# Batched x·yᵀ over 96 heads: all loads first, then 24 stores of four heads, and matmuls of 64 columns

## The chip, the cores and the metric

The kernel runs on one core of one Trainium2 chip. The time is the device time of one execution in microseconds. Before the change it is 300.93 us, the median of 3 runs (300.91 to 301.05).

The core has a matrix engine (PE, its weight loads are shown as PEld), a vector engine (DVE), a scalar engine (ACT), a general engine (POOL), an engine that here only issues transfers (SP), and 16 DMA engines that move data between DRAM and the on-chip memory. Matmul results arrive in PSUM, and DVE or ACT copies them from there.

## The reference

```
x, y: [batch 8, heads 12, 512, channels 64], float32
out = einsum('bhtc,bhsc->bhts', x, y)          # [8, 12, 512, 512], float32
```

For each of the 96 heads a 512x64 matrix is multiplied by the transpose of another. The inputs are 12.6 MB each and the output is 100.7 MB.

## The kernel before

**Tiling.** The 96 heads are taken in NG = 6 groups of G = 16 heads. A group of x (or y) is one load of 2 MB into a slot of 128 partitions x 4096 float32; there are five such slots (SLOTS), which hold the loads first and the results later. Load number n is x of group n/2 for even n, and y for odd n: 12 loads in all. Each group is worked on in two halves of eight heads (NH = 12 halves, numbered i = 2g + half), and each half gives four results of two heads (result, o = 4i + h): 128 partitions x 8 rows x 512 columns, 2 MB, written by one store in rows of 16 KB. There are 48 stores.

**From a load to the matmul's operands.** Everything that follows is counted in bfloat16.
- compress(n) for x: ACT casts the whole slot into a buffer xk (line 113 of the helper copy).
- compress(n) for y: four casts of 64 partitions x 2048 elements into the buffers yb, two for each half. The list in_front gives their engines: DVE and POOL for the first half, DVE and ACT for the second (line 150).
- mix(i, name, part): four copies of 32 partitions x 2048 from xk into xb. In xb two neighbouring 16-bit columns belong to different heads, and each partition fills only one of the two; the other keeps the zero of a memset made once. So one contraction over all 128 partitions yields rows of two heads, each with its own channels. There is one xb for each half (xbs, line 64).
- transposes(i): DVE transposes xb to xT and yb to yT in blocks of 32x32 (lines 178 and 188). There are two buffers of each, one for each half.
- result(o): for each of two groups of four rows (k = 0 and 4) four matmuls of 128 columns by 512 into a PSUM tile pm of four banks (line 202), and one copy of 128x2048 from pm to the slot (line 113), on ACT except in the two results named in late, where DVE makes it.
- store(o): issued by SP, or by ACT for every third result and for the last four (by_act).

**Order and waits.** The program is written out by hand. emit notes for each buffer who wrote and who read it last and adds the semaphore waits that follow; each engine and each DMA queue works strictly in its own order, so that what stands behind a waiting instruction waits too. The front (lines 246 to 271) issues five loads, then goes through the 12 loads and compresses each; POOL makes one mix copy after each of them (12 in all, for i = 0, 1, 2). Later loads follow when a slot is free, the first four results are put between the last loads, and afterwards prepare makes the transposes of half i and the mix of half i + 1 on DVE while the results of earlier halves are stored.

Of the kernel before, what the change touches and what calls it, by code (L numbers as in the profile page):

```python
# [9 lines left out]
def kernel(  # L10
# [22 lines left out]
    nc = tc.nc  # L33
    B, H, T, C = x.shape
    _, _, S, _ = y.shape
    P = 128
    G = 16
    Q = P // G
    R = T // Q
    NG = B * H // G  # L40
    NH = 2 * NG
    V = G // 4
    K = 8
    E = R // K
    D = 32
    SLOTS = 5
    fp32 = mybir.dt.float32
    bf16 = mybir.dt.bfloat16
    u32 = mybir.dt.uint32
    COPY = mybir.ActivationFunctionType.Copy  # L50
    assert C == 2 * D and S == T and R == 2 * D and Q * V == D

    xv = x.rearrange("b h t c -> (b h t c)").rearrange("(g p n) -> g p n", p=P, n=R * C)
    yv = y.rearrange("b h t c -> (b h t c)").rearrange("(g p n) -> g p n", p=P, n=R * C)
    ov = out.rearrange("b h t s -> (b h t s)").rearrange(
        "(o u h q n) -> o h q u n", u=2, h=V, q=Q * E, n=K * S
    )

    sb = ctx.enter_context(tc.tile_pool(name="sb", bufs=1))
    ps = ctx.enter_context(tc.tile_pool(name="ps", bufs=1, space=bass.MemoryType.PSUM))  # L60
    slots = [sb.tile([P, K * S], fp32, name=f"slot{i}") for i in range(SLOTS)]
    xks = [sb.tile([P, R, C], bf16, name=f"xk{i}") for i in range(NG - 1)]
    ybs = [[sb.tile([P, R // 2 * D], u32, name=f"yb{h}{i}") for i in range(NG - 1 + h)] for h in range(2)]
    xbs = [sb.tile([P, K * E * D], u32, name=f"xb{half}") for half in range(2)]
    xTs = [sb.tile([P, K * D * E], u32, name=f"xT{i}") for i in range(2)]
    yTs = [sb.tile([P, D * R // 2], u32, name=f"yT{i}") for i in range(2)]
    pms = [ps.tile([P, 4, S], fp32, name=f"pm{i}") for i in range(2)]
# [3 lines left out]
    def need(name, points):  # L71

        best = {}
        for p, v in points:
            if known[name].get(p, 0) < v:
                best[p] = max(best.get(p, 0), v)
        for p, v in list(best.items()):
            if any(snaps[q, w].get(p, 0) >= v for q, w in best.items() if q != p):
                del best[p]
        for p, v in best.items():  # L80
            engines[name].wait_ge(sems[p], v)  # L81
            known[name][p] = v
            for q, w in snaps[p, v].items():
                known[name][q] = max(known[name].get(q, 0), w)
# [19 lines left out]
        for w in writes:  # L104
            writer[w], readers[w] = at, []

    made_slots, loaded, later, late = [], {}, [], (V * NH - V - 1, V * NH - 1)
    in_front = ["dve", "pool", "dve", "act"]

    def copy(name, dst, src, reads, writes):  # L110
        emit(
            name,
            lambda: nc.scalar.activation(dst, src, COPY)  # L113
            if name == "act"
            else engines[name].tensor_copy(dst, src),  # L115
            reads,
            writes,
        )

    def both(i):  # L120
        return [("slot", i, 0), ("slot", i, 1)]

    def slot():
        made_slots.append(len(made_slots) % SLOTS)
        return made_slots[-1]

    def load(n):
        i = loaded[n] = slot()
        emit(
            "sp",  # L130
            lambda: nc.sync.dma_start(slots[i], (yv if n % 2 else xv)[n // 2]),  # L131
            writes=both(i),
            dma=i,
        )

    def compress(n):

        i = loaded.pop(n)
        g = n // 2
        if n % 2 == 0:  # L140
            xk = g % (NG - 1)
            dst = xks[xk].rearrange("p r c -> p (r c)")
            copy("act", dst, slots[i], both(i), [("xk", xk)])
            return
        ys = slots[i].rearrange("p (r c) -> p r c", c=C)
        for half in range(2):
            b = g % (NG - 1 + half)
            yv2 = ybs[half][b].bitcast(bf16).rearrange("p (j c w) -> p j w c", j=R // 2, w=2)
            for ch in range(2):
                copy(  # L150
                    in_front[2 * half + ch],
                    yv2[ch * 64:(ch + 1) * 64],
                    ys[half * 64:(half + 1) * 64, :, ch * D:(ch + 1) * D].rearrange(
                        "p (j w) c -> p j w c", w=2
                    ),
                    both(i),
                    [("yb", half, b, ch)],
                )

    def mix(i, name, part):  # L160

        g, half = divmod(i, 2)
        ch, u = divmod(part, 2)
        lo = half * 64 + u * D
        xk = g % (NG - 1)
        xv2 = xbs[half].bitcast(bf16).rearrange("p (k e c u) -> p k e c u", k=K, e=E, u=2)
        copy(
            name,
            xv2[part * D:(part + 1) * D, :, :, :, u],
            xks[xk][lo:lo + D, :, ch * D:(ch + 1) * D].rearrange("p (e k) c -> p k e c", k=K),  # L170
            [("xk", xk)],
            [("xb", half, part)],
        )

    def transposes(i):
        g, half = divmod(i, 2)
        b = g % (NG - 1 + half)
        emit(
            "dve",
            lambda: nc.vector.transpose(  # L180
                xTs[half].rearrange("p (k r e) -> p k e r", k=K, e=E),
                xbs[half].rearrange("p (k e c) -> p k e c", k=K, e=E),
            ),
            [("xb", half, part) for part in range(4)],
            [("xT", half)],
        )
        emit(
            "dve",
            lambda: nc.vector.transpose(  # L189
                yTs[half].rearrange("p (r j) -> p j r", r=D),  # L190
                ybs[half][b].rearrange("p (j c) -> p j c", c=D),
            ),
            [("yb", half, b, ch) for ch in range(2)],
            [("yT", half)],
        )

    def products(o, k):
        i, h = divmod(o, V)
        xT = xTs[i % 2].bitcast(bf16).rearrange("p (k h m) -> p k h m", k=K, h=V)
        yT = yTs[i % 2].bitcast(bf16)  # L200
        for j in range(4):
            last = nc.tensor.matmul(  # L202
                pms[k // 4][:, j, :], xT[:, k + j, h, :], yT[:, h * S:(h + 1) * S],
                start=True, stop=True,
            )
        return last

    def by_act(o):
        return o % 3 == 2 or o >= V * NH - V

    def store(o, s):
        i, h = divmod(o, V)
        name = "act" if by_act(o) else "sp"
        emit(
            name,
            lambda: engines[name].dma_start(ov[i, h], slots[s]),
            reads=both(s),
            dma=s,
        )

    def result(o, s):

        ot = slots[s].rearrange("p (r s) -> p r s", s=S)
        for k in range(0, K, 4):
            pm = k // 4
            half = o // V % 2
            emit("pe", lambda: products(o, k), [("xT", half), ("yT", half)], [("pm", pm)])
            copy("dve" if o in late else "act", ot[:, k:k + 4, :], pms[pm], [("pm", pm)], [("slot", s, pm)])
            if k == 0:
                while later:  # L230
                    store(*later.pop())
        if by_act(o):
            later.append((o, s))
        else:
            store(o, s)

    def prepare(i):

        if i < NH:
            transposes(i)  # L240
        if i + 1 < NH:
            for part in range(4):
                mix(i + 1, "dve", part)

    with tc.tile_critical():  # L245
        for g in range(SLOTS):
            load(g)
        for half, name in enumerate(("dve", "pool")):
            emit(
                name,  # L250
                lambda: engines[name].memset(xbs[half], 0.0),  # L251
                writes=[("xb", half, part) for part in range(4)],
            )
        front = []
        for n in range(2 * NG):
            if n == 11:
                result(3, slot())
            compress(n)
            mix(n // 4, "pool", n % 4)
            if n == 4:  # L260
                transposes(0)
            if n < 5:
                load(n + SLOTS)
            elif n in (6, 8):
                load(n // 2 + 7)
            elif n < 10:
                front.append(slot())
            if n > 7 and n < 11:
                result(n - 8, front[n - 8])
            if n == 9:  # L270
                transposes(1)
        prepare(2)
        for o in range(V, V * NH):
            result(o, slot())
            if o % V == V - 1:
                prepare(o // V + 2)
        store(*later.pop())
        for i, name in enumerate(("dve", "pool", "dve", "pe", "act")):
            need(name, [(f"dma{i}", ticks[f"dma{i}"])])


# [28 lines left out]
```

## Time and profile before

| what | value |
|---|---|
| device time, median of 3 runs | 300.93 us |
| span of the profiled execution, first to last instruction | 299.3 us |
| PE busy (384 matmuls) | 131.2 us, 44% |
| DVE busy | 160.8 us, 54% |
| ACT busy | 204.2 us, 68% |
| POOL busy | 56.0 us, 19% |
| DMA | 125.90 MB, 421 GB/s over the span |

The page gives the busy time of each engine as a share of the span; the 40 slices give it in tenths by time, with what the DMA engines moved. The groups give the mean time of one instruction and what ended the idle time before it. Names such as xT<-xb stand for the buffers written and read, without their numbers. The profiled execution is known by its span alone; its device time isn't recorded, and the median of the runs lies 1.6 us above that span.

The bytes are 25.17 MB read and 100.66 MB written. Loads take place from the start to about 63 us, stores from 55 us to the end.

### The profile page before, as it was taken

To read this page: it belongs to the slowest core of one execution; us is meant where nothing else is said; L and a number is where in the kernel's file an instruction comes from. 1 tells how busy PE (TensorE), PEld (TensorE's weight loads), DVE (VectorE), ACT (ScalarE), POOL (GpSimd) and SP (SyncE) were. 2 spreads that over 40 slices of the span, in tenths; PEclk is the share of its full clock that TensorE was granted. 3 is DMA by queue.
4 is the path that set the end of the run, shared out by engine and by line. 5 is a ranking of instruction groups with operands and counts; after the bars stand their busy time and mean duration, and the time that the engine had idled before them with its cause. 6 is when DMAs were issued, how large, how long until landed. Compare 5 with 4: busy or idle time off the path is not lost.

```text
span 299.3 us, 1170 instructions
## 1 busy us (share of the span) xinstructions
PE 131.2 (44%) x384; PEld 35.2 (12%) x384; DVE 160.8 (54%) x77; ACT 204.2 (68%) x105; POOL 56.0 (19%) x23
## 2 busy tenths in 40 slices
PE   0000040557756665454655545464646473755100
PEld 0000010111111111111111111111111111111000
DVE  2167897999839590940946729219276330501400
ACT  1665676999999885677776868595959595459000
POOL 2399999991000000000000000000000000000000
PEclk9999999999599978596859597959597959587755
DMA  7999999999999999999999999999999999999995
GB/s 272 429 427 434 431 425 427 429 431 427 434 434 429 429 431 428 431 434 431 427 434 428 429 434 429 429 427 436 425 425 429 427 434 423 425 423 429 431 431 239
DMA packets 8645, 125.90 MB, mean 421 GB/s; under 512 B 960, under 2 KB 960, under 8 KB 960
## 3 DMA queue, kind: packets, MB, share of 16 engines
q1 hardware_dynamic: 6048, 88.08, 69.3%
q10 hardware_dynamic: 2592, 37.75, 29.6%
q8 instruction: 3, 0.05, 0.1%
q14 instruction: 2, 0.02, 0.0%
HBM read 25.17 MB, written 100.66 MB: 420 GB/s over the span
## 4 chain that ended last, share of the span: by engine, by line
DMA 57%; ACT 22%; PE 7%; issue 4%; DVE 3%; SPq 0%; ACTq 0%
DMA out_dram<-slot 44%; ACT slot L113 19%; DMA slot<-in_y_dram 7%; PE pm L202 7%; DMA slot<-in_x_dram 6%; DVE yb L115 2%; DVE slot L115 1%; ACT xk L113 1%; ACT yb L113 1%; SPq L131 0%; ACTq L81 0%; SPq L305 0%; SPq L245 0%
## 5 line engine op out<-in xcount | busy, mean ns | idle before, releaser
L113 ACT ACTIVATE slot<-pm 128x2048 f32<-128x2048 f32 x92 | 166.6, 1883 | 50.1 <-DMA out_dram<-slot 40.8
L202 PE MATMUL pm<-yT,xT 128*128 128x512 bf16 x384 | 131.2, 485 | 146.6 <-ACT slot L113 108.6
L180 DVE STREAM_TRANSPOSE xT<-xb 128x2048 uint32<-128x2048 uint32 x12 | 46.7, 3890 | 71.0 <-PE pm L202 68.6
L202 PEld LDWEIGHTS pm<-yT,xT 128*128 128x128 bf16 x384 | 35.2, 112 | 242.1 <-ACT slot L113 141.4
L115 DVE COPY xb<-xk 32x2048 bf16<-32x2048 bf16 x36 | 46.9, 1304 | 1.0
L115 DVE CAST yb<-slot 64x2048 bf16<-64x2048 f32 x12 | 36.1, 3012 | 17.0 <-DMA slot<-in_y_dram 16.8
L115 POOL COPY xb<-xk 32x2048 bf16<-32x2048 bf16 x12 | 36.2, 3019 | 10.5 <-ACT xk L113 9.7
L113 ACT ACTIVATE xk<-slot 128x4096 bf16<-128x4096 f32 x6 | 21.7, 3617 | 16.4 <-DMA slot<-in_x_dram 16.4
L115 DVE COPY slot<-pm 128x2048 f32<-128x2048 f32 x4 | 9.0, 2286 | 29.3 <-PE pm L202 29.3
L189 DVE STREAM_TRANSPOSE yT<-yb 128x1024 uint32<-128x1024 uint32 x12 | 23.2, 1932 | 0.0
L113 ACT ACTIVATE yb<-slot 64x2048 bf16<-64x2048 f32 x6 | 14.8, 2461 | 5.1 <-DMA slot<-in_y_dram 5.1
L115 POOL CAST yb<-slot 64x2048 bf16<-64x2048 f32 x6 | 17.8, 2968 | 1.3 <-DMA slot<-in_y_dram 0.8
L251 DVE MEMSET xb<- 128x2048 uint32 x1 | 1.8, 1765 | 1.4 <-SPq L245 1.4
L251 POOL MEMSET xb<- 128x2048 uint32 x1 | 1.8, 1804 | 0.5 <-SPq L245 0.5
L113 ACT ACT_TABLE_LOAD x1 | 1.3, 1283 | 0.9 <-SPq L245 0.9
L294 POOL MEMSET const-float32-0.0<- 128x1 f32 x1 | 0.1, 98 | 0.2 <-issue 0.2
L294 POOL MEMSET const-float32-1.0<- 128x1 f32 x1 | 0.1, 98 | 0.0
L294 POOL MEMSET const-bfloat16-1.0<- 128x1 bf16 x1 | 0.1, 98 | 0.0
L294 POOL MEMSET const-uint8-127<- 128x1 uint8 x1 | 0.1, 97 | 0.0
## 6 DMA issues: line engine op xcount, KB each, us to landing
out_dram<-slot SPq DMA_DIRECT2D x30, 2048.0 KB, 17.0
out_dram<-slot ACTq DMA_DIRECT2D x18, 2048.0 KB, 14.8
slot<-in_x_dram SPq DMA_DIRECT2D x6, 2048.0 KB, 17.6
slot<-in_y_dram SPq DMA_DIRECT2D x6, 2048.0 KB, 20.8
```

Of the source, the lines that this page charges most:

```text
L113: lambda: nc.scalar.activation(dst, src, COPY)
L115: else engines[name].tensor_copy(dst, src),
L180: lambda: nc.vector.transpose(xTs[half].rearrange("p (k r e) -> p k e r", k=K, e=E), xbs[half].rearrange("p (k e c) -> p k e c", k=K, e=E),),
L189: lambda: nc.vector.transpose(yTs[half].rearrange("p (r j) -> p j r", r=D), ybs[half][b].rearrange("p (j c) -> p j c", c=D),),
L202: last = nc.tensor.matmul(pms[k // 4][:, j, :], xT[:, k + j, h, :], yT[:, h * S:(h + 1) * S], start=True, stop=True,)
L251: lambda: engines[name].memset(xbs[half], 0.0),
L294: nc = _bacc.Bacc("TRN2", target_bir_lowering=False, num_devices=1)
```

## The change

- A slot now has 128 x 8192 float32 (4 MB) and there are three. A load takes half a slot (load(n, place), six places); six loads are issued at once, the others follow by hand, each into a place whose casts are done. All 12 stand ahead of the first store on SP.
- A result covers four heads (t = 2i + z, 24 in all): 16 rows of 512 on each partition, so that a store writes rows of 32 KB. All stores are issued by SP. A result is made of four quarters of four rows.
- The rows of a half are split by K = 16 instead of 8. A quarter is eight matmuls: for each of its four banks one of 64 columns into partitions 0 to 63 and one into 64 to 127, for two pairs of heads (products).
- There is one xb for both halves. mix(0) is made by DVE, mix(1) and mix(2) by POOL, all others by DVE. All 96 quarter copies are ACT's.
- x and y are transposed by two functions, turn_x and turn_y, that can be placed apart.

The core of the diff, with the new functions:

```diff
@@ -40,28 +40,29 @@
     NG = B * H // G
     NH = 2 * NG
     V = G // 4
-    K = 8
+    K = 16
     E = R // K
     D = 32
-    SLOTS = 5
+    BIG = 3
+    NT = 2 * NH
     fp32 = mybir.dt.float32
     bf16 = mybir.dt.bfloat16
     u32 = mybir.dt.uint32
     COPY = mybir.ActivationFunctionType.Copy
-    assert C == 2 * D and S == T and R == 2 * D and Q * V == D
+    assert C == 2 * D and S == T and R == 2 * D and Q * V == D and K * S == 2 * R * C
 
     xv = x.rearrange("b h t c -> (b h t c)").rearrange("(g p n) -> g p n", p=P, n=R * C)
     yv = y.rearrange("b h t c -> (b h t c)").rearrange("(g p n) -> g p n", p=P, n=R * C)
     ov = out.rearrange("b h t s -> (b h t s)").rearrange(
-        "(o u h q n) -> o h q u n", u=2, h=V, q=Q * E, n=K * S
+        "(i u z p n) -> i z p u n", u=2, z=2, p=P // 2, n=K * S
     )
 
     sb = ctx.enter_context(tc.tile_pool(name="sb", bufs=1))
     ps = ctx.enter_context(tc.tile_pool(name="ps", bufs=1, space=bass.MemoryType.PSUM))
-    slots = [sb.tile([P, K * S], fp32, name=f"slot{i}") for i in range(SLOTS)]
+    slots = [sb.tile([P, K * S], fp32, name=f"slot{i}") for i in range(BIG)]
     xks = [sb.tile([P, R, C], bf16, name=f"xk{i}") for i in range(NG - 1)]
-    ybs = [[sb.tile([P, R // 2 * D], u32, name=f"yb{h}{i}") for i in range(NG - 1 + h)] for h in range(2)]
-    xbs = [sb.tile([P, K * E * D], u32, name=f"xb{half}") for half in range(2)]
+    ybs = [sb.tile([P, R // 2 * D], u32, name=f"yb{i}") for i in range(2 * NG - 3)]
+    xb = sb.tile([P, K * E * D], u32, name="xb")
     xTs = [sb.tile([P, K * D * E], u32, name=f"xT{i}") for i in range(2)]
     yTs = [sb.tile([P, D * R // 2], u32, name=f"yT{i}") for i in range(2)]
     pms = [ps.tile([P, 4, S], fp32, name=f"pm{i}") for i in range(2)]
@@ -104,8 +105,8 @@
         for w in writes:
             writer[w], readers[w] = at, []
 
-    made_slots, loaded, later, late = [], {}, [], (V * NH - V - 1, V * NH - 1)
     in_front = ["dve", "pool", "dve", "act"]
+    where, filled = {}, [0]
 
     def copy(name, dst, src, reads, writes):
         emit(
@@ -117,166 +118,194 @@
             writes,
         )
 
-    def both(i):
-        return [("slot", i, 0), ("slot", i, 1)]
...
-        i = loaded[n] = slot()
+    def load(n, place):
+        where[n] = place
+        s, half = divmod(place, 2)
         emit(
             "sp",
-            lambda: nc.sync.dma_start(slots[i], (yv if n % 2 else xv)[n // 2]),
-            writes=both(i),
...
-    def mix(i, name, part):
+            lambda: nc.sync.dma_start(
+                slots[s][:, half * R * C:(half + 1) * R * C], (yv if n % 2 else xv)[n // 2]
+            ),
+            writes=[("slot", s, 2 * half), ("slot", s, 2 * half + 1)],
+            dma=place,
+        )
+
+    def held(n):
+        s, part = divmod(where[n], 2)
+        return slots[s][:, part * R * C:(part + 1) * R * C], [("slot", s, 2 * part), ("slot", s, 2 * part + 1)]
+
+    def keep_x(n):
+        src, reads = held(n)
+        xk = n // 2 % len(xks)
+        copy("act", xks[xk].rearrange("p r c -> p (r c)"), src, reads, [("xk", xk)])
+
+    def home(g, half):
+
+        if half == 0:
+            return g % (NG - 1)
+        return 1 if g == NG - 1 else NG - 1 + g % (NG - 2)
+
+    def keep_y(n, half):
+        src, reads = held(n)
+        ys = src.rearrange("p (r c) -> p r c", c=C)
+        b = home(n // 2, half)
+        yv2 = ybs[b].bitcast(bf16).rearrange("p (j c w) -> p j w c", j=R // 2, w=2)
+        for ch in range(2):
+            copy(
+                in_front[2 * half + ch],
+                yv2[ch * 64:(ch + 1) * 64],
+                ys[half * 64:(half + 1) * 64, :, ch * D:(ch + 1) * D].rearrange(
+                    "p (j w) c -> p j w c", w=2
+                ),
+                reads,
+                [("yb", b, ch)],
+            )
+
+    def mix(i, name, parts=range(4)):
 
         g, half = divmod(i, 2)
-        ch, u = divmod(part, 2)
-        lo = half * 64 + u * D
...
-        b = g % (NG - 1 + half)
+        xk = g % len(xks)
+        xv2 = xb.bitcast(bf16).rearrange("p (k e c u) -> p k e c u", k=K, e=E, u=2)
+        for part in parts:
+            ch, u = divmod(part, 2)
+            lo = half * 64 + u * D
+            copy(
+                name,
+                xv2[part * D:(part + 1) * D, :, :, :, u],
+                xks[xk][lo:lo + D, :, ch * D:(ch + 1) * D].rearrange("p (e k) c -> p k e c", k=K),
+                [("xk", xk)],
+                [("xb", part)],
+            )
+
+    def turn_x(i):
+        half = i % 2
         emit(
             "dve",
             lambda: nc.vector.transpose(
                 xTs[half].rearrange("p (k r e) -> p k e r", k=K, e=E),
-                xbs[half].rearrange("p (k e c) -> p k e c", k=K, e=E),
+                xb.rearrange("p (k e c) -> p k e c", k=K, e=E),
             ),
-            [("xb", half, part) for part in range(4)],
+            [("xb", part) for part in range(4)],
             [("xT", half)],
         )
+
+    def turn_y(i):
+        g, half = divmod(i, 2)
+        b = home(g, half)
         emit(
             "dve",
             lambda: nc.vector.transpose(
                 yTs[half].rearrange("p (r j) -> p j r", r=D),
-                ybs[half][b].rearrange("p (j c) -> p j c", c=D),
+                ybs[b].rearrange("p (j c) -> p j c", c=D),
             ),
-            [("yb", half, b, ch) for ch in range(2)],
+            [("yb", b, ch) for ch in range(2)],
             [("yT", half)],
         )
 
-    def products(o, k):
-        i, h = divmod(o, V)
+    def products(t, k, pm):
+        i, z = divmod(t, 2)
         xT = xTs[i % 2].bitcast(bf16).rearrange("p (k h m) -> p k h m", k=K, h=V)
         yT = yTs[i % 2].bitcast(bf16)
         for j in range(4):
-            last = nc.tensor.matmul(
-                pms[k // 4][:, j, :], xT[:, k + j, h, :], yT[:, h * S:(h + 1) * S],
-                start=True, stop=True,
-            )
+            for w in range(2):
+                h = 2 * z + w
+                last = nc.tensor.matmul(
+                    pms[pm][w * 64:(w + 1) * 64, j, :],
+                    xT[:, k + j, h, :],
+                    yT[:, h * S:(h + 1) * S],
+                    start=True,
+                    stop=True,
+                )
         return last
 
-    def by_act(o):
-        return o % 3 == 2 or o >= V * NH - V
...
-
+    def quarter(t, s, k, name):
+        pm = filled[0] % 2
+        filled[0] += 1
+        half = t // 2 % 2
         ot = slots[s].rearrange("p (r s) -> p r s", s=S)
-        for k in range(0, K, 4):
-            pm = k // 4
...
-                mix(i + 1, "dve", part)
+        emit("pe", lambda: products(t, k, pm), [("xT", half), ("yT", half)], [("pm", pm)])
+        copy(name, ot[:, k:k + 4, :], pms[pm], [("pm", pm)], [("slot", s, k // 4)])
+
+    def store(t, s):
+        i, z = divmod(t, 2)
+        emit(
+            "sp",
+            lambda: nc.sync.dma_start(ov[i, z], slots[s]),
+            reads=[("slot", s, part) for part in range(4)],
+            dma=2 * s,
+        )
 
     with tc.tile_critical():
-        for g in range(SLOTS):
-            load(g)
...
-            need(name, [(f"dma{i}", ticks[f"dma{i}"])])
+        for n in range(2 * BIG):
+            load(n, n)
+        emit(
+            "dve",
+            lambda: nc.vector.memset(xb, 0.0),
+            writes=[("xb", part) for part in range(4)],
+        )
+        keep_x(0)
+        mix(0, "dve")
+        turn_x(0)
+        keep_y(1, 0)
+        keep_y(1, 1)
+        turn_y(0)
+        keep_x(2)
+        load(6, 2)
+        mix(1, "pool", range(1))
+        keep_y(3, 0)
+        keep_y(3, 1)
+        load(7, 3)
+        mix(1, "pool", range(1, 4))
+        turn_x(1)
+        keep_x(4)
+        load(8, 4)
+        quarter(0, 0, 0, "act")
+        keep_y(5, 0)
+        keep_y(5, 1)
+        load(9, 5)
+        turn_y(1)
+        quarter(0, 0, 4, "act")
+        keep_x(6)
+        load(10, 2)
+        quarter(0, 0, 8, "act")
+        mix(2, "pool", range(1))
+        keep_y(7, 0)
+        keep_y(7, 1)
+        load(11, 3)
+        quarter(0, 0, 12, "act")
+        store(0, 0)
+        mix(2, "pool", range(1, 4))
+        keep_x(8)
+        quarter(1, 2, 0, "act")
+        keep_y(9, 0)
+        keep_y(9, 1)
+        quarter(1, 2, 4, "act")
+        keep_x(10)
+        quarter(1, 2, 8, "act")
+        quarter(1, 2, 12, "act")
+        store(1, 2)
+        keep_y(11, 0)
+        turn_y(2)
+        quarter(2, 1, 0, "act")
+        quarter(2, 1, 4, "act")
+        keep_y(11, 1)
+        quarter(2, 1, 8, "act")
+        quarter(2, 1, 12, "act")
+        store(2, 1)
+        turn_x(2)
+        mix(3, "dve")
+        for t in range(3, NT):
+            s = (0, 2, 1)[t % 3]
+            for k in range(0, K, 4):
+                quarter(t, s, k, "act")
+            store(t, s)
+            i = t // 2 + 2
+            if t % 2 and i < NH:
+                turn_y(i)
+                turn_x(i)
+                if i + 1 < NH:
+                    mix(i + 1, "dve")
+        need("sp", [(f"dma{i}", ticks[f"dma{i}"]) for i in range(0, 2 * BIG, 2)])
 
 
 # ---- launch: one core; inputs and outputs as the reference has them ----
```

More of the change, by code (lines that the diff above doesn't have):

```diff
@@ L118, in copy @@
         )
-    def both(i):
-        return [("slot", i, 0), ("slot", i, 1)]
[L123 to L127, printed above, removed]
-        i = loaded[n] = slot()
+    def load(n, place):
+        where[n] = place
+        s, half = divmod(place, 2)
         emit(
             "sp",
-            lambda: nc.sync.dma_start(slots[i], (yv if n % 2 else xv)[n // 2]),
-            writes=both(i),
-            dma=i,
-        )
[L136 to L146, printed above, removed]
-            b = g % (NG - 1 + half)
[L148 to L157, printed above, removed]
-                )
@@ L160, in mix @@
-    def mix(i, name, part):
-        g, half = divmod(i, 2)
-        ch, u = divmod(part, 2)
-        lo = half * 64 + u * D
[L165 to L173, printed above, removed]
@@ L175, in transposes @@
-    def transposes(i):
-        g, half = divmod(i, 2)
-        b = g % (NG - 1 + half)
+            lambda: nc.sync.dma_start(
[3 more added lines that the diff above has]
+            dma=place,
+        )
+    def held(n):
+        s, part = divmod(where[n], 2)
+        return slots[s][:, part * R * C:(part + 1) * R * C], [("slot", s, 2 * part), ("slot", s, 2 * part + 1)]
@@ L201, in products @@
         for j in range(4):
-            last = nc.tensor.matmul(
-                pms[k // 4][:, j, :], xT[:, k + j, h, :], yT[:, h * S:(h + 1) * S],
-                start=True, stop=True,
-            )
-        return last
-    def by_act(o):
-        return o % 3 == 2 or o >= V * NH - V
-    def store(o, s):
-        i, h = divmod(o, V)
-        name = "act" if by_act(o) else "sp"
+            for w in range(2):
[7 more added lines that the diff above has]
+                )
@@ L214, in store @@
+        return last
+    def quarter(t, s, k, name):
+        pm = filled[0] % 2
+        filled[0] += 1
+        half = t // 2 % 2
+        ot = slots[s].rearrange("p (r s) -> p r s", s=S)
+        emit("pe", lambda: products(t, k, pm), [("xT", half), ("yT", half)], [("pm", pm)])
+        copy(name, ot[:, k:k + 4, :], pms[pm], [("pm", pm)], [("slot", s, k // 4)])
+    def store(t, s):
+        i, z = divmod(t, 2)
         emit(
-            name,
-            lambda: engines[name].dma_start(ov[i, h], slots[s]),
@@ L217, in store @@
-            reads=both(s),
-            dma=s,
-        )
-    def result(o, s):
-        ot = slots[s].rearrange("p (r s) -> p r s", s=S)
-        for k in range(0, K, 4):
-            pm = k // 4
[L226 to L242, printed above, removed]
-                mix(i + 1, "dve", part)
-    with tc.tile_critical():
-        for g in range(SLOTS):
-            load(g)
[L248 to L278, printed above, removed]
-            need(name, [(f"dma{i}", ticks[f"dma{i}"])])
```

## The prediction

> **What bounds the kernel now.** I read the page first: span, the slices, the DMA packets.
>
> ```profile
> span 299.3 us, 1170 instructions
> ...
> DMA  7999999999999999999999999999999999999995
> GB/s 272 429 427 434 431 425 427 429 431 427 434 434 429 429 431 428 431 434 431 427 434 428 429 434 429 429 427 436 425 425 429 427 434 423 425 423 429 431 431 239
> DMA packets 8645, 125.90 MB, mean 421 GB/s; under 512 B 960, under 2 KB 960, under 8 KB 960
> ```
>
> The 16 DMA engines are busy in every slice but the first and the last. 125.9 MB at 430 GB/s is 292.8 us; the other 6.5 us are start and end. The windows view says the same of the stretches: 429 GB/s from 10 to 55 us (loads only) and 430 from 100 to 250 us (stores only). So two things alone can move the time: what a byte costs on the DMA engines, and whether their queue ever runs dry. PE at 44%, DVE at 54% and ACT at 68% matter only through the second.
>
> Next, the front, where the new order is written out. The timeline of 8 to 56 us (start us, length us), rows of ACT, POOL and DVE:
>
> ```profile
> 8.81 3.62 ACT L113 ACTIVATE xk<-slot 128x4096 bf16<-128x4096 f32 x1 [6.63 <-DMA slot<-in_x_dram]
> ...
> 12.49 2.44 POOL L115 COPY xb<-xk 32x2048 bf16<-32x2048 bf16 x1 [9.75 <-ACT xk L113]
> ...
> 13.69 5.83 DVE L115 CAST yb<-slot 64x2048 bf16<-64x2048 f32 x2 [10.48 <-DMA slot<-in_y_dram]
> 15.06 3.29 POOL L115 CAST yb<-slot 64x2048 bf16<-64x2048 f32 x1
> ...
> 36.77 13.71 DVE L115 CAST yb<-slot 64x2048 bf16<-64x2048 f32 x4
> ...
> 43.05 2.44 ACT L113 ACTIVATE yb<-slot 64x2048 bf16<-64x2048 f32 x1 [1.27 <-DMA slot<-in_y_dram]
> ...
> 47.94 3.62 ACT L113 ACTIVATE xk<-slot 128x4096 bf16<-128x4096 f32 x1 [2.45 <-DMA slot<-in_x_dram]
> ...
> 52.85 4.78 DVE L115 CAST yb<-slot 64x2048 bf16<-64x2048 f32 x2 [2.36 <-DMA slot<-in_y_dram]
> ```
>
> Two readings. Whoever waits on the DMA starts at 8.81, 13.69, ... 43.05, 47.94, 52.85: a load lands every 4.89 us. And DVE and POOL hold each other up. By tile, the casts and copies take:
>
> ```profile
> L115 DVE CAST yb<-slot x12: 1320/3401/3452, 13.7 to 66.3; 64x2048 bf16<-64x2048 f32 x12
> ...
> L115 DVE COPY xb<-xk x36: 1267/1305/1329, 76.2 to 228.2; 32x2048 bf16<-32x2048 bf16 x36
> L115 POOL COPY xb<-xk x12: 2439/3384/3459, 12.5 to 65.2; 32x2048 bf16<-32x2048 bf16 x12
> ```
>
> (shortest/median/longest ns). Alone, DVE needs 1.32 and POOL 2.45 us; side by side each shows 3.4. They alternate: POOL's copy ends at 14.93, its cast at 18.35, and DVE's two casts at 19.52, 1.17 after POOL's. So in a mixed stretch POOL ends 2.3 us after DVE's operation and DVE 1.15 after POOL's. Transposes don't take part: xT<-xb keeps 3.9 us beside POOL.
>
> **The change part by part.** *Bytes.* The same 125.9 MB. Output rows become 32 KB, 24 stores for 48: per DMA engine 192 rows where there were 384, and 24 completion packets fewer. The packet records behind the page give 611 ns for a 16 KB row, 307 ns at best for an 8 KB one and 9 ns for a completion. 2x307-611 = 3 ns is the fixed part: 192x3 ns + 24x9 ns = 0.8 us saved per engine. At the other end nothing is saved, if 32 KB moves as two pieces. I take -0.8.
>
> [...]
>
> *One queue.* Before, ACT issued 18 stores and SP 30. In the load stretch SP alone kept 429 GB/s, so one queue is enough: 0. ACT loses 18 issues of 0.55 us; SP only issues.
>
> *Evictions.* All 96 on ACT at 1.88 us, plus six keep_x of 3.62 and six casts of 2.45: 217 us of 300. A 4 MB store lasts 9.76 us on the DMA engines and is filled by 4x1.88 = 7.5 us of ACT. With three slots, the fill of one slot overlaps the stores of the other two; hidden with about 10 us of slack in the steady part. If that cover went, ACT at 7.5 against 9.76 would still keep up.
>
> *Matmuls.* 768 of 64 columns for 384 of 128, 512 rows each. The trace has no pair in two halves of a bank. Bounds: both halves at once (PE as now), or one after the other (twice). Per quarter of a store that is 8 matmuls. Four took 1.04 us at 265.92 and about 1.9 us at the low clock (124.00 in the chain), so a quarter lies between 1.04 and 3.8 us; the limit for hiding is 9.76/4 = 2.44. I take hidden: one after the other at the good clock is 2.1, and a PE that is always busy has in this trace the higher clock (0.5 is granted at 285 to 290 us with no matmul, 0.80 in 100 to 250).
>
> [...] The trace's weight loads are 112 ns beside matmuls of 485; even twice as long, an estimate from that row, they stay beside them.
>
> *The front.* Here the order changes most. DVE now makes mix(0) (four copies), xb is one buffer, so POOL's mix(1) must wait for turn_x(0) to have read it, and mix(2) for turn_x(1). Loads go into half slots: load 7 needs keep_y(3) done, load 8 keep_x(4), load 9 keep_y(5), load 11 keep_y(7). SP issues in order, so what is behind a waiting load waits too. With the durations above:
> - ACT keep_x(0) ends 12.43. DVE's mix(0): first copy to 13.8; POOL's cast of y0 (landed 13.69) to 16.1; second copy 17.2; two alone to 19.9. turn_x(0) to 23.85.
> - DVE casts y0: 25.0; POOL mix(1) part 0: 27.3; DVE 28.4; POOL's cast of y1: 30.7. DVE turns y0 beside it, to 30.4.
> - DVE casts y1: 31.9; POOL part 1: 34.2; DVE 35.3 (load 7 is issued here; its queue is still full until about 37); POOL parts 2 and 3: 37.6, 40.1.
> - turn_x(1) waits for part 3: 40.1 to 44.1. It is the new wait, and behind it on DVE stand the casts of y2 for which load 9 waits.
> - DVE's first cast of y2 begins at 43.9 (an operation starts 0.2 before a transpose's recorded end, as 36.77 against 36.97) and ends 45.2. POOL's mix(2) part 0 has waited since 44.1 (keep_x(6) on ACT ends 42 to 44): 47.5. DVE's second cast: 48.7. Load 9 is issued at 48.7.
>
> Unbroken, load 9 would land at 52.85. Issued into a dry queue it lands no sooner than 1.0 (issue to first byte: 0.95 to 1.9 at the start) + 4.89 later, at 54.6: +1.8. By the only other load issued into an empty queue, the first (0.95 to 8.81, 7.86 us), it lands at 56.6: +3.7. The first 5 us ran 0.9 us short of full rate, part of which I put down to a program's first transfer; I take +2.8.
>
> Load 10 follows at once; load 11 needs keep_y(7): POOL cast 50.9, DVE 52.0, POOL 54.2, DVE 55.5, while load 10 runs to about 59: no second hole. Store 0 is filled by then. Store 1 needs POOL's last cast of y4 (64.6) and two evictions: issued 68.5, due at 73. Store 2 at 78.4, due at 82.8. From store 3 on the slack grows.
>
> Sum against the profiled execution: 299.3 + 2.8 - 0.8 = 301.3 us. The median of the runs, 300.93, lies 1.6 above that span; with it the forecast is 302.9 us.
>
> **The rivals.** *No hole (faster).* It decides at 46.0: the queue runs dry near 47.0 (load 8 lands at 47.94), 1.0 less for the issue. If DVE's chain is 2.7 us earlier, load 9 costs nothing and the saving remains: 300.93 - 0.8 = 300.1. For it: uncontended operations alone would put the issue at 41. Against it: between 36.45 and 52.8 DVE and POOL alternated without exception.
>
> *PE too slow.* Pairs one after the other at the low clock: 3.7 us a quarter, 14.8 a store against 9.76. Each store lost costs 5.0 until the clock rises; two of them, less the slack of 4.4 at store 2, plus the hole: 300.93 + 2.8 + 10 - 4.4 = 309.3. Point: a quarter of over 2.44 us. Against: PE would be busy throughout.
>
> *POOL goes twice before DVE's second cast* (mix(2) part 0, then its cast of y3): load 9 at 52.1, +3.4: 306.3.
>
> *The stores don't profit.* The DMA engines are already full; included as S = 0, 303.7.
>
> **How the numbers follow.** A difference under about 0.2%, 0.6 us, can't be told from none. The hole 0.62 (1.8 to 3.7, less 0 to 0.8, so 301.9 to 304.6; a tenth of this case, with a shorter hole, within 0.6 of before), no hole 0.25 (299.5 to 300.7, mostly faster), PE 0.06, POOL twice 0.07. Faster 0.23, same 0.10, slower 0.67. Its own range is 301.0 to 304.6; to hold 8 in 10 with both signs: 299.6 to 305.0.
>
> **What would show it.** In the profile after: a slice or window near 47 to 50 us with DMA below 9; on SP a load waiting for a DVE cast of yb, issued near 48.7; DVE's xT waiting on POOL's xb near 37 to 40; a POOL COPY of 3.4 us between the two casts of y2; all stores on one queue, 24 issues; after 70 us DMA 9 throughout and ACT waiting for DMA. Wrong would be: no gap at 47, PE's wait at the stores, or a store rate away from 430 GB/s.

## The result and the profile after

The changed kernel takes 305.84 us (median of 5 runs, 305.63 to 306.26) against 300.93: a ratio of 1.0161, 95% interval 1.0149 to 1.0174. It is 4.9 us slower. The forecast was 302.9 with 299.6 to 305.0: the right direction, and less than half of the loss.

The page of the changed kernel, its span, slices and DMA queues:

```profile
span 303.8 us, 1880 instructions
...
DMA  7999996999999999999999999999999999999992
GB/s 272 427 436 425 423 427 227 431 414 438 427 423 444 436 429 423 441 428 431 429 444 423 427 440 436 425 427 444 431 427 429 440 431 423 444 429 427 431 444 125
DMA packets 5192, 125.95 MB, mean 415 GB/s; under 512 B 576, under 2 KB 576, under 8 KB 576
...
q1 hardware_dynamic: 5184, 125.83, 97.1%
q8 instruction: 6, 0.10, 0.1%
```

One slice in the front shows 227 GB/s: the hole. The last slice shows 125 where the kernel before had 239. Between them the rate is as before or a little above it. The hole in windows (stretch and length in us; busy us and instructions of PE, weight loads, DVE, ACT and POOL; granted clock, DMA share, GB/s):

```profile
40.00:45.00 5.00, 1.51 (x10) 0.45 (x8) 4.85 (x2) 4.97 (x3) 3.44 (x3) 0.50 1.00 426
45.00:50.00 5.00, 2.54 (x14) 0.65 (x10) 4.94 (x3) 4.95 (x3) 4.87 (x2) 0.50 0.58 203
50.00:55.00 5.00, 1.30 (x8) 0.45 (x8) 4.97 (x3) 3.91 (x2) 4.87 (x3) 0.50 0.88 351
55.00:60.00 5.00, 0.98 (x6) 0.10 (x2) 4.27 (x3) 3.58 (x2) 4.94 (x2) 0.50 1.01 433
100.00:250.00 150.00, 89.85 (x494) 29.25 (x492) 82.67 (x44) 112.29 (x63) 0.00 (x0) 0.77 1.00 432
```

The timeline shows what load 9 waited for (start us, length us; rows of DVE, then POOL, then SP):

```profile
40.15 3.88 DVE L184 STREAM_TRANSPOSE xT<-xb 128x2048 uint32<-128x2048 uint32 x1 [4.88 <-POOL xb L116]
43.88 4.77 DVE L116 CAST yb<-slot 64x2048 bf16<-64x2048 f32 x2
...
40.25 2.48 POOL L116 CAST yb<-slot 64x2048 bf16<-64x2048 f32 x1
44.16 3.33 POOL L116 COPY xb<-xk 32x2048 bf16<-32x2048 bf16 x1 [1.43 <-DVE xT L184]
...
35.30 0.33 SPq L126 DMA_DIRECT2D slot<-in_y_dram  x1
...
48.67 0.33 SPq L126 DMA_DIRECT2D slot<-in_y_dram  x1
49.04 0.43 SPq L126 DMA_DIRECT2D slot<-in_x_dram  x1
55.72 0.33 SPq L126 DMA_DIRECT2D slot<-in_y_dram  x1
```

DVE idles 4.88 us for POOL's mix copies, transposes from 40.15, and then needs 4.77 us for two casts: 1.30 for the first and 3.44 for the second, which POOL's copy (44.16 to 47.49) overlaps. The shortest of these casts before took 1.32. Load 9 is issued at 48.67, when load 8 (landed 47.93) has nothing behind it. The page counts 576 packets under 512 B, 16 for each of the 36 transfers; a load is taken as landed when the last of its 16 completions is signalled. Load 9 lands at 56.37, where the kernel before has 52.82: 3.55 us late. Load 11 lands at 66.89 against 62.59, 4.30 us late.

The matmuls behave well. The first 16 of 64 columns, two quarters, in the timeline of PE:

```profile
30.33 3.36 PE L212 MATMUL pm<-yT,xT 128*64 128x512 bf16 x16 [30.33 <-DVE yT L197]
```

Before, the first eight of 128 columns:

```profile
37.03 3.59 PE L202 MATMUL pm<-yT,xT 128*128 128x512 bf16 x8 [37.03 <-DVE yT L189]
```

The granted clock was 1.00 in both stretches. So a pair of 64 columns cost what one of 128 did, and the two of a pair start within 5 ns of each other: the two halves of a bank run at the same time.

So the hole is there, but load 11 is 4.3 us late and the kernel loses 4.9, although the long rows should give something back. The theory to test had three parts: the late loads cost more than the one landing, the long rows save more than 0.8 us, and something costs at the end of the span.

### The profile page after: what moved, and what is told of

It is laid out like the page before. It is cut to its first block, busy times and chain, and to the rows that moved or that the text cites. A ratio compares the mean times of both kernels' runs of the same rounds, so it can differ in the third digit from the quotient of the medians.

```text
span 303.8 us, 1880 instructions
## 1 busy us (share of the span) xinstructions
PE 141.6 (47%) x768; PEld 45.8 (15%) x768; DVE 154.0 (51%) x77; ACT 213.1 (70%) x109; POOL 45.2 (15%) x18
## 4 chain that ended last, share of the span: by engine, by line
DMA 51%; ACT 18%; POOL 12%; PE 5%; DVE 5%; issue 1%; ACTq 0%; POOLq 0%; SPq 0%
DMA out_dram<-slot 49%; ACT slot L114 15%; POOL xb L116 9%; PE pm L212 5%; POOL yb L116 3%; DVE xT L184 3%; DMA slot<-in_x_dram 3%; DVE xb L116 2%; ACT xk L114 1%; ACT yb L114 1%; ACTq L82 0%; POOLq L82 0%; SPq L334 0%; SPq L238 0%
## 5 line engine op out<-in xcount | busy, mean ns | idle before, releaser
L114 ACT ACTIVATE slot<-pm 128x2048 f32<-128x2048 f32 x96 | 175.4, 1876 | 49.9 <-DMA out_dram<-slot 44.1
L212 PE MATMUL pm<-yT,xT 128*64 128x512 bf16 x768 | 141.6, 516 | 137.5 <-ACT slot L114 106.7
L212 PEld LDWEIGHTS pm<-yT,xT 128*64 128x64 bf16 x768 | 45.8, 137 | 232.3 <-ACT slot L114 156.9
L116 DVE COPY xb<-xk 32x2048 bf16<-32x2048 bf16 x40 | 55.6, 1389 | 10.4 <-ACT xk L114 9.2
L184 DVE STREAM_TRANSPOSE xT<-xb 128x2048 uint32<-128x2048 uint32 x12 | 46.0, 3836 | 4.9 <-POOL xb L116 4.9
L116 DVE CAST yb<-slot 64x2048 bf16<-64x2048 f32 x12 | 29.0, 2413 | 5.1 <-DMA slot<-in_y_dram 4.9
L116 POOL COPY xb<-xk 32x2048 bf16<-32x2048 bf16 x8 | 26.3, 3284 | 9.6 <-DVE xT L184 9.2
L116 POOL CAST yb<-slot 64x2048 bf16<-64x2048 f32 x6 | 18.8, 3126 | 15.6 <-DMA slot<-in_y_dram 15.1
```

What stands on the lines that cost most here:

```text
L184: lambda: nc.vector.transpose(xTs[half].rearrange("p (k r e) -> p k e r", k=K, e=E), xb.rearrange("p (k e c) -> p k e c", k=K, e=E),),
L212: last = nc.tensor.matmul(pms[pm][w * 64:(w + 1) * 64, j, :], xT[:, k + j, h, :], yT[:, h * S:(h + 1) * S], start=True, stop=True,)
```

## The experiments

Every time is a median, and the kernel before, run beside them, had 300.88 to 301.09 us.

**1. Move the transpose that makes load 9 late.** If load 9 is the cause, a single moved line gives its time back.

```diff
         mix(1, "pool", range(1, 4))
-        turn_x(1)
         keep_x(4)
...
         load(9, 5)
+        turn_x(1)
         turn_y(1)
```

> The changed kernel with one line moved: turn_x(1) stands behind the casts of y2 and the issue of load 9 instead of ahead of them, so that DVE casts y2 while POOL still makes mix(1). Theory (the late load 9 makes the hole of 47 to 50 us): load 9 is issued near 44.6 us instead of 48.67, lands near 52.9 instead of 56.37, no stretch of the front has a DMA share below 9 tenths, and the time falls by the 3.5 us of the late landing, to about 302.4 us. Rival (the loss lies in the stores or at the end, and the hole only comes out of slack that is there anyway): not more than 1 us is given back, 305 us.

The window from 45 to 50 us:

```profile
45.00:50.00 5.00, 2.47 (x14) 0.74 (x10) 5.00 (x3) 4.95 (x3) 3.21 (x2) 0.50 0.96 403
```

Measured: 303.40 us (302.48 to 304.26; ratio to before 1.0080, 1.0065 to 1.0095). Load 9 was issued at 44.99, the DMA share from 45 to 50 us rose from 0.58 to 0.96, and 2.4 us came back, two thirds of what was expected. In the profile, taken of the slowest of these runs, load 9 still landed at 54.33, 1.5 us late, and load 11 at 64.73, 2.1 late. The rival, at most 1 us, falls. But an issue 3.3 us ahead of load 8's landing (48.26) wasn't enough. Why isn't shown: in the changed kernel load 7 was issued only 2.7 us ahead of load 6's landing (35.30 against 38.04) and landed on time (43.04; before, 43.02).

**2. The opposite: load 9 still later.**

```diff
         quarter(0, 0, 0, "act")
+        turn_y(1)
         keep_y(5, 0)
         keep_y(5, 1)
         load(9, 5)
-        turn_y(1)
```

> The changed kernel with turn_y(1) moved ahead of the casts of y2, which makes load 9 later still: by the durations of the profile (transpose 2.0, POOL copy 2.45 beside it, then DVE and POOL in turn) it is issued near 51.1 us instead of 48.67. Theory (each microsecond that load 9 is late is a microsecond of the time): 2.4 us slower than the changed kernel, 308.2 us. Rival (the hole is paid out of slack): within 0.6 us of the changed kernel, 305.8 us.

Measured: 308.57 us (1.0256, 1.0241 to 1.0270), 2.7 us above the changed kernel. Load 9 was issued at 51.42, 2.75 us later. Each of these microseconds is paid in full; there is no slack.

**3. Short rows, with the moved transpose.**

```diff
-        emit(
-            "sp",
-            lambda: nc.sync.dma_start(ov[i, z], slots[s]),
-            reads=[("slot", s, part) for part in range(4)],
-            dma=2 * s,
-        )
+        for w in range(2):
+            cut = slice(w * R * C, (w + 1) * R * C)
+            emit(
+                "sp",
+                lambda: nc.sync.dma_start(ov[i, z][:, :, cut], slots[s][:, cut]),
+                reads=[("slot", s, part) for part in range(4)],
+                dma=2 * s + w,
+            )
...
```

> The kernel with turn_x(1) moved, and each 4 MB store split into two of 2 MB in rows of 16 KB, issued one behind the other by SP. It shows what the long rows are worth by themselves. Theory (a 32 KB row takes 1213 ns where two of 16 KB take 2 x 611, and the mean is 1215 against 2 x 613.5; 192 long rows per DMA engine): 1.7 to 2.3 us slower than the kernel with turn_x(1) moved alone, some 304.5 us. Rival (the rows' own cost is the 3 ns that the prediction took): 0.6 us slower; and if the 4 MB stores themselves cost at the end, this one is faster.

Measured: 303.80 us (303.37 to 305.76), 0.4 above experiment 1, inside the scatter of both. It decided nothing, and was repeated on a steadier kernel as experiment 9.

**4. Two queues, with the moved transpose.**

```diff
+        name = "act" if t % 2 else "sp"
         emit(
-            "sp",
-            lambda: nc.sync.dma_start(ov[i, z], slots[s]),
+            name,
+            lambda: engines[name].dma_start(ov[i, z], slots[s]),
...
```

> The kernel with turn_x(1) moved, and every second store issued by ACT instead of SP. Theory (one queue keeps the DMA engines full): within 0.5 us of the kernel with turn_x(1) moved alone, 302.4 us. Rival (the last DMA engine ends 2.8 us after the mean in the changed kernel against 1.6 before because one queue lets the engines drift apart): 1 us faster, 301.4 us, with the last DMA engine nearer to the others.

Measured: 303.12 us (302.46 to 303.25), within 0.3 of experiment 1. One queue is enough; the rival gets at most a small part.

**The end of the span.** In the packet records of experiment 1 the DMA engines send their last completions at 296.2 us on average, and one of them at 300.62. Before, these were 296.4 and 297.84. One engine is far behind the others. The last completion comes 4.4 us after the mean in experiment 1, 2.8 in the changed kernel and 1.5 before. A difference between the kernels that hits few packets is in the queue view: 6 instruction packets of 16 KB each. Before:

```profile
q8 instruction: 3, 0.05, 0.1%
```

The changed kernel has 768 matmuls with 768 weight loads instead of 384 and 384. The number of instruction packets doubles with them, so the theory was: PE's instructions are fetched by packets among the data, all on one DMA engine.

**5. Half the PE instructions.**

```diff
-        xT = xTs[i % 2].bitcast(bf16).rearrange("p (k h m) -> p k h m", k=K, h=V)
+        xT = xTs[i % 2].bitcast(bf16).rearrange("p (k z m) -> p k z m", k=K, z=2)
...
-            for w in range(2):
-                h = 2 * z + w
-                last = nc.tensor.matmul(
-                    pms[pm][w * 64:(w + 1) * 64, j, :],
-                    xT[:, k + j, h, :],
-                    yT[:, h * S:(h + 1) * S],
+            last = nc.tensor.matmul(
+                pms[pm][:, j, :],
+                xT[:, k + j, z, :],
+                yT[:, 2 * z * S:(2 * z + 1) * S],
...
```

> The kernel with turn_x(1) moved, but each pair of 64-column matmuls is one of 128 columns that multiplies both pairs of heads by the y of the first; the rows of the second pair of heads are therefore left uncomputed (they hold another product). 384 matmuls and weight loads instead of 768, the same evictions and the same transfers. Theory (the instruction packets of 16 KB, 6 in the changed kernel's DMA queues against 3 before, run on one DMA engine, which so ends last: mean end 296.2, last end 300.6 us): 3 packets, the last DMA engine ends near the others, 2.6 us faster than with 64 columns, 300.8 us. Rival (the late last engine comes from the long rows or the 4 MB stores): 303.4 us as with 64 columns.

Measured: 301.32 us (300.33 to 302.06), 2.1 us under experiment 1, with 3 instruction packets. The last DMA engine's completion came 1.9 us after the mean instead of 4.4. The rival, no change, falls. The second pair of heads isn't computed here, so this only prices the PE instructions.

**6. Twice the PE instructions, in the kernel before.** This leaves transfers, slots and order untouched.

```diff
         for j in range(4):
+            nc.tensor.matmul(
+                pms[k // 4][:, j, :8], xT[:, k + j, h, :], yT[:, h * S:h * S + 8],
+                start=True, stop=True,
+            )
             last = nc.tensor.matmul(
...
```

> The kernel before, with a matmul of 8 columns of y put ahead of each of its 384, into the same place, which the full one then overwrites: twice as many PE instructions, no change of transfers or of their order. PE has room (44% busy). Theory (instruction packets on one DMA engine): 6 instruction packets instead of 3, and 2.6 us more than before, 303.5 us. Rival (the number of PE instructions costs nothing as long as PE has room): 300.9 us.

The queue view of this kernel:

```profile
q8 instruction: 6, 0.10, 0.1%
```

Measured: 302.55 us (1.0055, 1.0043 to 1.0067), 1.6 us more than before. The direction is the theory's; the time rises by 0.55 us for each packet more, not 0.87. All loads landed within 0.05 us of those of the kernel before, so the loss is behind the front.

**7. Four times the PE instructions.** The same edit with three small matmuls ahead of each.

> The kernel before, with three matmuls of 8 columns ahead of each of its 384: four times as many PE instructions. Theory (with one small matmul each, 3 more instruction packets cost 1.64 us, 0.55 a packet, all on one DMA engine): 12 instruction packets, 9 more than before, 5 us more than before, 305.8 us. Rival (the 1.64 us came from something that grows otherwise, such as PE work or the end of the program): 301.5 to 303.5 us.

The queue view of this kernel:

```profile
q8 instruction: 12, 0.20, 0.2%
```

Measured: 306.15 us (1.0170, 1.0156 to 1.0184), 5.1 us above the kernel before run beside it: 0.56 us for each of 9 more packets. The cost follows the number of PE instructions, while PE is still only 51% busy. There is one packet for 256 PE instructions in every kernel here, so this run can't tell whether the packets are what costs.

**8. No late load at all.** POOL casts y2 and y4 before it mixes, and turn_x(1) moves behind load 11.

```diff
         load(6, 2)
-        mix(1, "pool", range(1))
         keep_y(3, 0)
         keep_y(3, 1)
         load(7, 3)
-        mix(1, "pool", range(1, 4))
-        turn_x(1)
...
         load(9, 5)
+        mix(1, "pool")
         turn_y(1)
...
-        mix(2, "pool", range(1))
         keep_y(7, 0)
         keep_y(7, 1)
         load(11, 3)
+        turn_x(1)
...
-        mix(2, "pool", range(1, 4))
...
         keep_y(9, 1)
+        mix(2, "pool")
```

> The changed kernel with POOL's mix(1) and mix(2) put behind its casts of y2 and y4 and turn_x(1) behind the issue of load 11, so that loads 7, 9 and 11 are issued near 33, 40 and 51 us. Theory (a load issued so late that its queue is almost dry costs too: with turn_x(1) moved load 9 was issued at 45.0 and landed at 54.33, load 11 at 64.73, against 52.82 and 62.59 before): loads 9 and 11 land within 0.3 us of the times before, and the time is 2 us under that of the kernel with turn_x(1) moved, 301.4 us. Rival (loads lose by the row length or the order of stores anyway): 303.4 us.

SP's issues in the timeline of this kernel:

```profile
32.90 0.33 SPq L126 DMA_DIRECT2D slot<-in_y_dram  x1
33.27 0.43 SPq L126 DMA_DIRECT2D slot<-in_x_dram  x1
38.08 0.33 SPq L126 DMA_DIRECT2D slot<-in_y_dram  x1
42.32 0.33 SPq L126 DMA_DIRECT2D slot<-in_x_dram  x1
52.53 0.33 SPq L126 DMA_DIRECT2D slot<-in_y_dram  x1
```

And two of its windows:

```profile
45.00:50.00 5.00, 2.54 (x14) 0.71 (x10) 4.97 (x2) 4.95 (x3) 4.80 (x3) 0.50 1.03 439
50.00:55.00 5.00, 1.30 (x8) 0.39 (x8) 4.97 (x3) 4.88 (x3) 4.60 (x2) 0.50 0.99 423
```

Measured: 301.60 us (301.52 to 301.90; 1.0024, 1.0014 to 1.0034). Load 9 is issued at 38.08 and lands at 52.82, load 11 at 62.60: to 0.01 us as before. The late loads together cost 305.84 - 301.60 = 4.2 us, close to the 4.30 by which load 11 was late.

**9. Short rows again, on the kernel of experiment 8.** The edit is that of experiment 3.

> The kernel with the casts first, with each 4 MB store split into two of 2 MB in rows of 16 KB issued one behind the other by SP. It prices the long rows where no load is late. Theory (192 long rows per DMA engine of 1213 ns against two of 611, 24 completions of 9 ns, and less scatter): 1.7 to 2.3 us slower than with the casts first, 303.3 to 303.9 us. Rival (3 ns per row, as the prediction took it): 0.8 us, 302.4 us. A second rival (the long rows give back at the end, by engines further apart, what they save): no difference, 301.6 us.

Measured: 302.93 us (302.78 to 303.06), 1.33 us above experiment 8. The kernel before had 301.09 beside this run and 300.91 beside experiment 8; with each taken against its own, the difference is 1.15. Long rows are worth 1.2 to 1.3 us: between the forecast's 0.8 and the 1.7 to 2.3 expected here. In the records a 32 KB row takes 1213 ns and a 16 KB row 611, so 9 ns are saved per pair, 192 x 9 = 1.7 us for an engine. The last engine is 3.1 us behind the mean with long rows and 2.4 with short ones; that may be what takes back part of it.

**10. No late load and half the PE instructions.** The edits of experiments 8 and 5 together; the second pair of heads again holds another product.

> The kernel with the casts first and one 128-column matmul for each pair (the second pair of heads again holds another product). Theory (hole and instruction packets are all that the change loses, and the long rows give about 2 us): 298.8 us, 2.1 under the kernel before. Rival (the long rows' gain doesn't reach the end): 300.9 us.

The queue view of this kernel:

```profile
q8 instruction: 3, 0.05, 0.1%
```

Measured: 299.85 us (0.9968, 0.9956 to 0.9979), 1.75 us under experiment 8 and 1.1 us under the kernel before, midway between the 298.8 of the theory and the 300.9 of its rival. It shows what the long rows would be worth if they didn't need matmuls of 64 columns; it isn't a kernel for the task. No kernel that computes everything beat the one before; experiment 8 comes nearest, 0.24% above it.

**Not one engine with all the packets.** The packet records settle part of what experiments 5 to 7 leave open. In experiment 8 an instruction packet takes 0.88 to 1.05 us, and the row that its DMA engine sends next 1.58 to 1.63 us instead of 1.21: 1.3 to 1.4 us in all. Six of these on one engine would be about 8 us, but the last engine ended only 3.1 us after the mean. So the packets don't all go to one engine, and that part of the theory is wrong.

The records show something else that grows with the PE instructions. Between 66 and 278 us, 137 of the 2791 rows of 32 KB in experiment 8 take 5 to 61 ns longer than 1213; almost all follow one another as the rows of a single engine would, and they add up to 3.97 us. With half the PE instructions, in experiment 10, there are 137 such rows again, no two at the same time, and they add up to 2.35 us. After 278 us, when the matmuls are over, no row of either is above 1215 ns. The 1.6 us between the two kernels is near the 1.75 of their times. So the cost of the PE instructions is measured; that slowed rows on one engine carry it is argued from these sums, and what slows them isn't known.

The account: 300.93 before, -1.33 for the long rows (experiment 9 against 8), +1.75 for twice the PE instructions (8 against 10; 1.64 by experiment 6), +4.24 for the late loads (the changed kernel against 8). The sum is 305.59, with 0.25 us left of the measured 305.84. The last two terms lead from experiment 10 to the changed kernel by construction; what the sum tests is whether the long rows alone explain the 1.08 us between the kernel before and experiment 10.

## Why the prediction was right or wrong

**The front, step by step: right.** The chain of DVE and POOL was forecast to issue load 9 at 48.7; it was 48.67. Load 7 was forecast at 35.3 (35.30), load 11 at 55.5 (55.72). The alternation of DVE and POOL read from the rows of before held up to there. *No hole* and *POOL goes twice* are out.

**The price of the hole: mis-sized.** The step "I take +2.8" failed in size. The bounds were +1.8 and +3.7. Load 9 landed 7.70 us after its issue, almost as the first load (7.86), so the landing was +3.55 late: the upper end, the only row of an issue into an empty queue, was nearer. I had put part of its length down to a program's first transfer; here an empty queue in mid-program cost nearly as much.

**"No second hole": right, and not enough.** The queue didn't run dry again, yet load 11 landed 5.62 us after load 10 instead of 4.89, and 4.30 us late in all. In the records its rows are slower: the mean of 16 KB rows is 652 ns from 46 to 62 us, the restart included, against 616 in that stretch before, and 721 for the rows that start after 62 us. With all loads issued early (experiment 8) this went away too. The sum had no term for it, and it makes the price of the hole +4.24 instead of +2.8. Why load 11's rows are slow stays open: its issue was 5.5 us ahead of load 10's landing, and in experiment 8 a lead of 5.2 us was enough.

**The bytes: mis-sized.** "I take -0.8" measured -1.33. The 3 ns came from 8 KB packets at their best, which the records have on an instruction queue (q14) and which aren't data rows. The rows of the changed kernel give 1213 - 611 = 602 ns for the second 16 KB, which leaves 9 ns per row. With 24 completions of 9 ns, that is an estimated saving of 1.9 us for an engine, above the 1.33 that reached the end.

**The matmuls: the step "I take hidden" failed.** PE did have room (47% busy), and the pairs run at the same time; *PE too slow* is out. But 768 more PE instructions cost 1.75 us (experiment 8 against 10), in a kernel whose DMA engines are the limit (share 1.00 from 100 to 250 us in both). That cost was nowhere in the sum: the step counted only PE's time, although the sentence that "two things alone can move the time" asked what the matmuls do to the DMA engines, and the page of before listed the instruction packets. 768, 1536 and 3072 PE instructions gave 3, 6 and 12 packets of 16 KB here, one for 256. A packet took its DMA engine 1.3 us and more; how much of the 0.55 us of time for each 256 instructions comes from that isn't shown. That a PE that is always busy has the higher clock isn't shown either: before, 0.50 was granted from 124 to 126 us with PE busy throughout, and 1.00 over the first 75 us with PE busy for 17.3 of them.

**Evictions, one queue, later stores: right.** Stores 1 and 2 were issued at 68.9 and 79.1 (forecast 68.5 and 78.4) without a gap, and experiment 4 found no gain in a second queue.

With the measured sizes the forecast's sum would have been 300.93 + 4.24 - 1.33 + 1.75 = 305.6.

## What to carry to other kernels

In these kernels, which keep all DMA engines busy, PE's instructions had a price though PE had room (44 to 51% busy): 0.55 us for 256 (experiments 6 and 7). Count them before doubling them. The load issued into a dry queue cost its wait and a slow start, 7.70 us to landing where 4.89 lie between loads in a full queue, and the nearest price was the first load of the program, 7.86 to its cast. Put on an engine's queue first what frees a buffer for a transfer, and behind it what only feeds a later stage: here turn_x(1), waiting for POOL, stood on DVE ahead of the casts of y2 (load 5, landed at 33.15), which began at 43.88.

## What the runs showed of the hardware

- With the DMA engines full (share 1.01 from 100 to 250 us before and in experiment 6), more PE instructions cost time: 1.64 us for 768 more (experiment 6) and 5.06 us for 2304 more (experiment 7), about 0.55 us for 256. With 3072 of them the last DMA engine ended 5.1 us after the mean, with 768 it was 1.5.
- An instruction packet of 16 KB came with each 256 of them (3, 6 and 12 for 768, 1536 and 3072) and cost its DMA engine 1.3 us or more (experiment 8: 0.88 to 1.05 us, and 0.37 to 0.41 on the next row; the changed kernel: 0.88 to 0.96, and 0.37 to 0.41), where a 16 KB row of data takes 0.61. The six of experiment 8 don't all go to the engine that ends last: it ended 3.1 us after the mean, where six would be about 8 us.
- Two matmuls of 64 columns into the two halves of a bank start together, within 5 ns in the first eight pairs: 16 took 3.36 us where 8 of 128 columns took 3.59, both at a granted clock of 1.00.
- A 2 MB load issued into an empty queue landed 7.70 us later (load 9 of the changed kernel; 7.86 to its cast for the first load before), where loads in a full queue land every 4.89. How far ahead it must be issued isn't clear: 3.3 us ahead of load 8's landing (experiment 1), load 9 landed 1.5 us late; 9.8 us ahead (experiment 8), it was not late; but load 7 of the changed kernel, 2.7 us ahead, wasn't late either.
